# A two-layer mixer in float32: the first layer's second block multiplied plainly, with its y kept on chip

## The chip, the cores and the metric

The kernel runs on one core of one Trainium2 chip. The metric is device time in microseconds (us), lowest is best; the median of three runs of the kernel before is 1554.78 us (1552.35 to 1556.88).

## The reference, cut to what matters

```
for l in range(2):                                  # x: (1, 2048, 1024), float32
    mod = silu(c) @ w_ada[l] + b_ada[l]             # 3 x 1024: shift, scale, gate
    h = rms_norm(x, g_pre[l]) * (1 + scale) + shift
    proj = h @ w_in[l]                              # 1024 x 3072
    u_a, b_a, c_a, gate_a, u_p, gate_p = six slices of proj, 512 wide
    y_a = b_a * conv3(c_a * u_a) * silu(gate_a)     # causal, depthwise
    y_p = pool(u_p, w_pool[l]) * silu(gate_p)       # causal means over 2, 4, 8, 16 tokens, then 128x128 each
    y = concat(y_a, y_p) @ w_out[l]                 # 1024 x 1024
    x = x + gate * rms_norm(y, g_post[l])
```

## The kernel before, in words

Everything is kept transposed: 128 channels on the partitions, tokens along the free axis. The 2048 tokens are two blocks of 1024, so with two layers there are four blocks, (layer, block) = (0,0), (0,1), (1,0), (1,1), done in that order. Each has an **input stage** (h by w_in, with convolution, pooling and gates behind it) and an **output stage** (y by w_out). Float32 operands are split into a high and a low part (float32r), and each product is made of three matmuls: high x high, high x low, low x high (`PASSES`).

- **Plain input stage**, `in_phase`, used for (0,0): 24 column groups of 128, each 8 K-tiles x 3 passes x 2 token halves of 512 = 48 matmuls, 1152 in all. Weights come in halves of four K-tiles; `Weights.load` issues the DMA (SP queue), `high` casts the high part on ACT, `settle` takes the low part on DVE. In turn k = 1 of a half, `settle` does the half that is used two halves later. y stays on chip.
- **Input stage with seven products**, `in_seven`, used for the other three blocks: two column groups, two halves of K and two token halves make a 2 x 2 by 2 x 2 product, done with seven products instead of eight (12 pairs x 7 products x 4 K-tiles x 3 passes = 1008 matmuls). It needs sums of weight quarters (S1 to S4), sums of quarters of h (B, T names), and sums of results on DVE. Its y goes to HBM (`yin`) and is read back. `settle` runs two products ahead.
- **Output stage**, `out_phase`: 384 matmuls; beside them the scaled results go to HBM (`ysp`), and the next block's h operands are prepared (`operands`); the last block has its own, `out_last`. What is left of the output's norm is done by `opening`, at the head of the next input stage: the mean of squares, then `rsqrt_steps` (Ln, Identity and Exp on ACT, three DVE steps of Newton) for each token half.

Beside the matmuls runs a list of background tasks, fed by `Paced`: each turn (8 turns to a column group in `in_phase`, one per product in `in_seven`) gives an equal share of the estimated DVE time of all tasks as credit. At most two tasks are active, and one more task's loads are issued ahead. The tasks are: `sum_task`, which reads the quarters of one weight unit, forms S1 to S4 with their high and low parts and writes them to HBM (`sums`), 24 for each layer; `mix_task`, which multiplies the pooling weights into w_in on PE (8 for each layer); `ada_task` (the conditioning product, on DVE); `x_stat_task` (sum of squares of x for the next block's norm); `finish_tasks` (16 for each block: x plus the normed y, for the block whose output stage has just ended).

Every engine executes its instructions in the order written, so a DVE instruction that waits for a DMA holds all DVE work written behind it. `in_phase` ends with `bg.drain()`: all tasks that are left are emitted before the next stage's first instruction.

```
            tasks += [sum_task(0, n, u, True) for n, u in units]
            tasks += [call_task(lambda: load_wpool(1), 0.1)]
            tasks += [sum_task(1, n, u, True) for n, u in mine("AB")[: 2 * EXTRA[0]]]
            tasks += [mix_task(1, g, n, later) for g in range(NCG) for n in range(2)]
            tasks += [x_stat_task(1, s, k, accs, later) for s in range(NH) for k in range(KT)]
```

These stand behind 6 mixes and 8 ada tasks in (0,0)'s list: 28 sums in all there. (0,1) has 16 finish tasks, 16 ada tasks and 12 sums of layer 1; (1,0) has 8 sums, 16 finish and 8 ada tasks; (1,1) has 16 finish tasks.

Of the kernel before, what the change touches and what calls it, by code (L numbers as in the profile page):

```python
# [10 lines left out]
ALU = mybir.AluOpType  # L11
# [18 lines left out]
EXTRA = (2, 6)  # L30
# [3 lines left out]
def trunk(ctx: ExitStack, tc: tile.TileContext, xt, c, wada, vec, rcp, win, wupt, wpool, wout, out):  # L34
# [305 lines left out]
    def x_stat_task(b, s, k, accs, later):  # L340
# [6 lines left out]
        def steps():  # L347
# [11 lines left out]
            if k == KT - 1:  # L359
                yield from stat_steps(accs.pop(s), (0, b, s), later)  # L360

        return load, steps, E2 * ((k > 0) + (k == KT - 1))
# [39 lines left out]
    def mix_task(l, g, n, later):  # L402
# [7 lines left out]
        def steps():  # L410
# [5 lines left out]
            yield 0.3  # L416
# [5 lines left out]
        return load, steps, 0.3  # L422
# [110 lines left out]
    def in_phase(l, b, hrhs, tasks, later, started, yplaces, wplaces):  # L533
# [70 lines left out]
        order = START_ORDER  # L604
        pss, wss, other_half = started
        first = len(wss)
        work = Work()
        mixes = [mix_task(l, 0, n, later) for n in range(2)]
        for load, _, _ in mixes:
            load()  # L610
        ws = Weights([w_src(l, *order[n], h) for n in range(first, len(order)) for h in range(2)], wplaces)
        uses = [use[order[n][0]](order[n][1], 0, HS, [pss[n]]) for n in range(first)]
        for _ in range(5):
            next(other_half)
        next(uses[0])
        next(uses[1])
        next(uses[2])
        for _ in other_half:
            pass
        for steps in uses:  # L620
            for _ in steps:
                pass
        for part in (range(0, 3), range(3, first)):
# [27 lines left out]
        bg = Paced(tasks, 1, 8 * (len(order) - first) - 6)  # L651
        for n in range(first, len(order)):
# [3 lines left out]
            for k in range(KT):  # L656
# [16 lines left out]
        return lambda k: y[k]  # L673
# [207 lines left out]
    def out_phase(l, b, y, nl, nb, ws, hplaces, lplaces):  # L881
# [61 lines left out]

        def evict(j, ps):
# [21 lines left out]
        ops = [operands(k) for k in range(KH)]  # L966
        ops[0][0]()
        nl_ = 0
        for j in range(KT):
            ps = [bank("ps_out") for _ in range(NH)]  # L970
            for n, k in enumerate(range(KT) if j else OUT_ORDER):
# [8 lines left out]
                if n == 6 and j < KH:  # L980
                    work.q.append(ops[j][1]())
                    if j + 1 < KH:
                        ops[j + 1][0]()
                work.run(free)
# [3 lines left out]
        spare = {}  # L988

        def fill(n, name, k, it=iter(lplaces)):  # L990
# [12 lines left out]
        fills = [fill(n, name, k) for n, name in enumerate(LATE) for k in range(KH)]  # L1003
# [14 lines left out]
        return h, fills, opening  # L1018
# [282 lines left out]

    with working(9, 4, 4, 3, 0):
        with tc.manual_schedule(engines={E.DVE, E.PE, E.Activation}):
            hrhs, started = start(0)
        with tc.manual_schedule():
            later = Later()
            tasks = [mix_task(0, g, n, later) for g in range(1, NCG) for n in range(2)]
# [119 lines left out]
```

## Time and profile before

| what | value |
|---|---|
| median of 3 runs | 1554.78 us |
| the profiled execution | 1560.83 us, span of its instructions 1559.1 us |
| busy, PE / DVE / ACT / POOL | 1403.5 / 1047.8 / 522.1 / 368.3 us |
| mean granted TensorE clock | 0.947 of full speed |
| HBM read / written | 259.09 / 104.33 MB |

The profiled execution lasts 1.7 us longer than its span and stands 6.05 us above the median. PE is TensorE with its matmuls, PEld its weight loads, DVE VectorE, ACT ScalarE, POOL GpSimd, SP the queue that issues most loads. "Busy" is the time in which an engine executes an instruction.

### The profile page before, as it was taken

How to read it: one execution, taken by the hardware profiler on the slowest of the kernel's cores; microseconds unless marked ns; L12 is line 12 of the kernel's file. 1: busy time of each engine (PE TensorE's matmuls, PEld its weight loads, DVE VectorE, ACT ScalarE, POOL GpSimd, SP SyncE). 2: the span in 40 equal slices, each digit the busy share in tenths (PEclk: the TensorE clock that was granted, in tenths of full speed). 3: DMA queues.
4: the chain of work that ended last, by engine and by line, in shares of the span. 5: the costliest groups of instructions: out<-in, count | busy, mean ns of one | idle time of the engine just before them, and what ended most of it. 6: DMA issues, size and time to landing. Idle time of an engine off the chain costs nothing. (4 is left out here: it accounts for less than half of the span.)

```text
span 1559.1 us, 18650 instructions
## 1 busy us (share of the span) xinstructions
PE 1403.5 (90%) x6100; PEld 1139.2 (73%) x6100; DVE 1047.8 (67%) x1763; ACT 522.1 (33%) x928; POOL 368.3 (24%) x535
## 2 busy tenths in 40 slices
PE   8899999945999999768899987999999899999996
PEld 4678888834877777546687776777788688888796
DVE  8954876845757778657675774877775656556555
ACT  4332434334544221222454521222364511112421
POOL 4500344350222221434022333221012122221000
PEclk9999999976999999889999999999999999999998
DMA  7407879786668999688666789878756788687513
GB/s 298 156 21 227 267 268 326 265 299 205 209 218 283 276 313 309 211 280 266 212 223 214 220 282 304 275 256 284 237 198 203 225 236 250 212 251 227 189 63 101
DMA packets 181668, 364.70 MB, mean 234 GB/s; under 512 B 20289, under 2 KB 48961, under 8 KB 181570
## 3 DMA queue, kind: packets, MB, share of 16 engines
q1 hardware_dynamic: 112178, 187.84, 37.0%
q0 software_dynamic: 69392, 175.67, 34.6%
q8 instruction: 48, 0.79, 0.2%
q14 instruction: 50, 0.41, 0.1%
HBM read 259.09 MB, written 104.33 MB: 233 GB/s over the span
## 5 line engine op out<-in xcount | busy, mean ns | idle before, releaser
L792 PE MATMUL ps_in<-h,ws 128*128 128x512 f32 x3024 | 729.2, 403 | 80.9 <-DVE ws L727 73.7
L792 PEld LDWEIGHTS ps_in<-h,ws 128*128 128x128 f32 x3024 | 587.6, 195 | 221.2 <-DVE ws L727 87.4
L388 PE MATMUL ps_out<-y,ws 128*128 128x512 f32 (+1 forms) x1728 | 355.7, 368 | 0.6 <-ACT ws L210 0.6
L388 PEld LDWEIGHTS ps_out<-y,ws 128*128 128x128 f32 x1728 | 300.5, 190 | 55.1 <-ACT ws L210 1.2
L388 PE MATMUL ps_in<-h,ws 128*128 128x512 f32 x816 | 185.9, 389 | 0.0
L388 PEld LDWEIGHTS ps_in<-h,ws 128*128 128x128 f32 x816 | 152.9, 188 | 31.6
L702 POOL DMA_DIRECT2D ws<-sums x144 | 103.7, 730 | 200.4 <-PE ps_in L792 184.7
L210 ACT CAST ws<-raw 128x512 fp32r<-128x512 f32 x98 | 60.1, 623 | 129.4 <-PE ps_out L388 48.6
L388 PE MATMUL ps_in<-h,w 128*128 128x512 f32 x336 | 86.7, 418 | 14.5 <-ACT h L377 8.0
L220 DVE TENSOR_TENSOR ws<-raw,ws 128x512 fp32r<-128x512 f32 x98 | 66.8, 688 | 48.2 <-ACT ws L210 48.1
L727 DVE TENSOR_TENSOR ws<-raw,ws 128x512 fp32r<-128x512 f32 x108 | 74.0, 686 | 29.2 <-ACT ws L717 29.2
L816 ACT COPY v<-ps_in 128x512 f32<-128x512 f32 x36 | 21.2, 590 | 213.1 <-PE ps_in L792 213.1
L388 PEld LDWEIGHTS ps_in<-h,w 128*128 128x128 f32 x336 | 66.8, 202 | 34.3 <-ACT h L377 11.6
L948 POOL DMA_DIRECT2D ysp<-yg x48 | 26.3, 547 | 275.3 <-ACT yg L947 275.3
L717 ACT CAST ws<-raw 128x512 fp32r<-128x512 f32 x108 | 63.1, 620 | 67.2 <-DMA raw<-win 35.0
L837 ACT ACTIVATE second<-second 128x1024 f32<-128x1024 f32 x24 | 25.5, 1062 | 149.5 <-DVE second L831 141.0
L474 POOL DMA_DIRECT2D sums<-raw x96 | 68.2, 773 | 3.9 <-DMA sums<-raw 2.0
L264 DVE SCALAR_TENSOR_TENSOR adaw<-adaw,cb 128x512 f32<-128x512 f32 x64 | 42.7, 688 | 33.6 <-DMA adaw<-wada 31.2
L472 POOL DMA_DIRECT2D sums<-s x48 | 35.4, 738 | 126.3 <-DVE s L467 118.8
L463 ACT CAST s13h<-s 128x512 fp32r<-128x512 f32 x48 | 29.8, 621 | 87.1 <-DVE s L458 41.7
L471 POOL DMA_DIRECT2D sums<-s13h x48 | 39.2, 816 | 72.2 <-ACT s13h L463 49.4
L457 DVE TENSOR_TENSOR s<-raw,raw 128x256 f32<-128x256 f32 x20 | 8.4, 421 | 56.3 <-DMA raw<-win 47.5
(174 smaller groups left out, 1494.9 us busy)
## 6 DMA issues: line engine op xcount, KB each, us to landing
ws<-sums POOLq DMA_DIRECT2D x144, 512.0 KB, 7.6
raw<-win SPq DMA_DIRECT2D x110, 256.0 KB, 5.3
sums<-raw POOLq DMA_DIRECT2D x96, 256.0 KB, 5.0
raw<-win SPq DMA_DIRECT2D x160, 128.0 KB, 4.4
adaw<-wada SPq DMA_DIRECT2D x64, 256.0 KB, 5.0
raw<-wout SPq DMA_DIRECT2D x64, 256.0 KB, 3.9
sums<-s13h POOLq DMA_DIRECT2D x48, 256.0 KB, 5.4
sums<-s POOLq DMA_DIRECT2D x48, 256.0 KB, 4.6
```

The lines of the kernel that those rows point to most:

```text
L210: nc.scalar.copy(self.ws[m][:, 0], self.raws[m].rearrange("p (a b) -> p a b", b=P))
L220: nc.vector.tensor_tensor(t[:, 1], raw, t[:, 0].bitcast(F32), op=ALU.subtract)
L264: nc.vector.scalar_tensor_tensor(w[n], w[n], 1.0, cb[:, n * HS : (n + 1) * HS], op0=ALU.mult, op1=ALU.mult, accum_out=m[:, l, j : j + 1])
L388: nc.tensor.matmul(ps[s], lhsT=ws[k // KH][:, wi, k % KH, :], rhs=rhs(k, ri, s), start=first and (wi, ri) == PASSES[0], stop=last and (wi, ...
L463: nc.scalar.copy(xh, xf)
L471: nc.gpsimd.dma_start(dst[:, 0, 0:4:2, cols].bitcast(F32), xh.bitcast(F32))
L472: nc.gpsimd.dma_start(dst[:, 1, 0:4:2, cols].bitcast(F32), xf)
L474: nc.gpsimd.dma_start(dst[:, :, 1 + 2 * m, cols].bitcast(F32), rs[m].bitcast(F32))
L702: nc.gpsimd.dma_start(ops[m].rearrange("p a b c -> p a (b c)"), sums[l, n][:, :, SUM[a]])
L717: nc.scalar.copy(ops[m][:, 0], raws[m].rearrange("p (a b) -> p a b", b=P))
L727: nc.vector.tensor_tensor(ops[m][:, 1], raw, ops[m][:, 0].bitcast(F32), op=ALU.subtract)
L792: nc.tensor.matmul(ps, lhsT=ops[m][:, wi, k, :], rhs=h[hn][k][:, ri, :], start=p < 4 and k == 0 and (wi, ri) == (0, 0), stop=k == KH - 1 a ...
```

## The change

1. (0,1)'s input stage becomes plain: `in_phase` instead of `in_seven`, so layer 0's 24 weight sums are not made, and y is not sent through HBM. `out_phase` gets a form `plain` in which (0,0)'s output stage prepares the plain h (`plain_operands`), and which fetches the first three weight halves of the input stage to come (`plain.high(3)`, `plain.settle`). `opening` is called in turns 0, 4 and 9 of `in_phase`, and background tasks start after turn 9.
2. Layer 1's sums: 16 (pairs A and B) in (0,0), 8 (pairs P) in (0,1), none in (1,0).
3. Layer 1's 8 mixes move from (0,0) to (0,1). (0,0)'s `x_stat_task`s stand among the sums instead of at the end, and their two means are tasks of their own (`x_stat_end`), with the matmuls five turns later (`later(5, mean)`).
4. In (1,0) the 8 ada tasks are spread between the 16 finish tasks.
5. The buffer pools of (0,0)'s output and (0,1)'s input stage: 8 wide, 6 half, 4 landing, 3 weight buffers; (0,1)'s output stage starts with the pools that `in_seven` uses.

```diff
@@ x_stat_task, stat_steps
-            if k == KT - 1:
-                yield from stat_steps(accs.pop(s), (0, b, s), later)
...
-        yield None
-        yield None
-        xstat[key] = mean_mm((ah, al))
+
+        def mean():
+            xstat[key] = mean_mm((ah, al))
+
+        later(5, mean)
+
+    def x_stat_end(b, s, accs, later):
+        return (lambda: None), (lambda: stat_steps(accs.pop(s), (0, b, s), later)), E2
@@ in_phase
-        bg = Paced(tasks, 1, 8 * (len(order) - first) - 6)
+        bg = Paced(tasks, 1, KT * (len(order) - first) - (10 if started else 20))
...
+                turn = KT * (n - first) + k
+                if opening and turn in (0, 4, 9):
+                    opening((0, 1, 3)[(0, 4, 9).index(turn)])
+                    free = 0
                 free = work.run(free)
-                if free > 0:
-                    bg.run(free + 1)
+                if not opening or turn > 9:
+                    bg.run(free + 1 if free > 0 else 0)
@@ out_phase
+            def steps():
+                t = xs[0]
+                nc.vector.scalar_tensor_tensor(t, t, apre[:, nl, k : k + 1], rn, op0=ALU.mult, op1=ALU.mult)
...
+                    nc.scalar.activation(hp0[s][k][:, 0], u, AF.Identity, bias=mod[:, nl, k : k + 1])
+                yield None
+                for d, u in parts:
+                    prenorm_lo(d[:, 0], d[:, 1], nl, k, u)
+                    yield E2
...
+                if plain and j == KT - 1 and n == 6:
+                    plain.high(3)
+                    plain.settle(2)
@@ the program
             tasks = [mix_task(0, g, n, later) for g in range(1, NCG) for n in range(2)]
-            tasks += [ada_task(0, 2 * KT + k) for k in range(KT)]
-            tasks += [call_task(lambda: ada_fin(0, 2, 0, KT), 0.3)]
-            tasks += [sum_task(0, n, u, True) for n, u in units]
+            rest = [ada_task(0, 2 * KT + k) for k in range(KT)]
+            rest += [call_task(lambda: ada_fin(0, 2, 0, KT), 0.3)]
+            rest += [x_stat_task(1, s, k, accs) for s in range(NH) for k in range(KT)]
+            tasks += between(rest, [sum_task(1, n, u, True) for n, u in mine("AB")])
+            tasks += [x_stat_end(1, s, accs, later) for s in range(NH)]
             tasks += [call_task(lambda: load_wpool(1), 0.1)]
-            tasks += [sum_task(1, n, u, True) for n, u in mine("AB")[: 2 * EXTRA[0]]]
-            tasks += [mix_task(1, g, n, later) for g in range(NCG) for n in range(2)]
-            accs = {}
-            tasks += [x_stat_task(1, s, k, accs, later) for s in range(NH) for k in range(KT)]
...
+    with working(8, 6, 4, 3, 0), tc.manual_schedule():
+        ws = out_weights(0, wplaces)
+        ws.load(3)
+        ws.settle(2)
+        first = in_weights(0, IN_ORDER, 0, wplaces[1:] + wplaces[:1])
+        hrhs, _, opening = out_phase(0, 0, y, 0, 1, ws, hplaces, None, first)
+        later = Later()
+        mixes = [mix_task(1, g, n, later) for g in range(NCG) for n in range(2)]
+        fins = finish_tasks(0, 0, later)
+        adas = [ada_task(1, j) for j in list(range(8, 16)) + list(range(8))]
+        adas += [call_task(lambda: (ada_fin(1, 1, 0, KT), ada_fin(1, 0, 0, KT)), 0.5)]
+        sums_ = [sum_task(1, n, u, True) for n, u in mine("P")]
+        tasks = between(mixes, fins[:4]) + between(between(adas, sums_), fins[4:])
+        y = in_phase(0, 1, hrhs, tasks, later, None, yplaces, first.places, first, opening)
...
-        for n, (l, b) in enumerate(blocks[1:], 1):
+        for n, (l, b) in enumerate(blocks[2:], 2):
...
             if (l, b) == (1, 0):
-                tasks = [sum_task(1, n_, u, False) for n_, u in sorted(rest)[2 * EXTRA[1] :]] + tasks
-                tasks += [ada_task(1, 2 * KT + k) for k in range(KT)]
+                tasks = between(tasks, [ada_task(1, 2 * KT + k) for k in range(KT)])
```

`between(many, few)` spreads the second list evenly through the first. Twenty-four sums are gone from the whole, and 144 matmuls are added.

Where the engines' instructions come to stand is seen in the order in which they are issued. First PE from (0,0)'s last products to (0,1)'s first ones, in the kernel before (ps_wu is a mix, ps_stat a mean, L388 and L792 the plain and the seven-product matmuls):

```order
L388 MATMUL ps_in<-h,ws 128x512 x798
L414 MATMUL ps_wu<-wp,wupt 128x128 x32
L309 MATMUL ps_stat<-ah,ones 128x512
L309 MATMUL ps_stat<-al,ones 128x512
L309 MATMUL ps_stat<-ah,ones 128x512
L309 MATMUL ps_stat<-al,ones 128x512
L388 MATMUL ps_out<-y,ws 128x512 x384
L792 MATMUL ps_in<-h,ws 128x512 x48
```

The same place now (L390 is the plain matmul, L308 the mean):

```order
L390 MATMUL ps_in<-h,ws 128x512 x750
L308 MATMUL ps_stat<-ah,ones 128x512
L308 MATMUL ps_stat<-al,ones 128x512
L390 MATMUL ps_in<-h,ws 128x512 x6
L308 MATMUL ps_stat<-ah,ones 128x512
L308 MATMUL ps_stat<-al,ones 128x512
L390 MATMUL ps_in<-h,ws 128x512 x30
L390 MATMUL ps_out<-y,ws 128x512 x384
L390 MATMUL ps_in<-h,ws 128x512 x60
```

The 32 mix matmuls (eight mixes) and the two means no longer stand between the last product and the output stage; the means stand 36 and 30 matmuls ahead of the end, the mixes among (0,1)'s products.

Second, ACT in `opening` of (1,0), at the head of its input stage (L287, L288 and L289 are Ln, Identity and Exp of one token half; L717 is the cast of a weight quarter, L829 a result). Before:

```order
L184 CAST ah<-acc 128x512 x2
L717 CAST ws<-raw 128x512 x2
L287 ACTIVATE rs_a<-ps_stat,epsc 128x512
L288 ACTIVATE rs_v<-ps_stat,epsc 128x512
L289 ACTIVATE ry<-rs_a 128x512
L287 ACTIVATE rs_a<-ps_stat,epsc 128x512
L288 ACTIVATE rs_v<-ps_stat,epsc 128x512
L289 ACTIVATE ry<-rs_a 128x512
L717 CAST ws<-raw 128x512
L829 COPY u<-ps_in 128x512
L837 ACT_TABLE_LOAD
```

Now (the same operations are L183, L729, L286, L287, L288, L841, L849):

```order
L729 CAST ws<-raw 128x512 x2
L286 ACT_TABLE_LOAD
L286 ACTIVATE rs_a<-ps_stat,epsc 128x512
L287 ACTIVATE rs_v<-ps_stat,epsc 128x512
L288 ACT_TABLE_LOAD
L288 ACTIVATE ry<-rs_a 128x512
L286 ACT_TABLE_LOAD
L286 ACTIVATE rs_a<-ps_stat,epsc 128x512
L287 ACTIVATE rs_v<-ps_stat,epsc 128x512
L288 ACT_TABLE_LOAD
L288 ACTIVATE ry<-rs_a 128x512
L729 CAST ws<-raw 128x512
```

Four loads of an activation table stand among the six activations, ahead of the cast of a weight quarter; before there was none.

Third, ACT where (0,1)'s input stage ends and its output stage begins, now (L599 is the Silu of the last gate, L544 the cast of its y, L209 the cast of an output weight, L875 the table load that `out_phase` asks for):

```order
L209 CAST ws<-raw 128x512 x2
L875 ACT_TABLE_LOAD
L599 ACT_TABLE_LOAD
L599 ACTIVATE sga<-ps_in 128x512 x2
L209 CAST ws<-raw 128x512
L544 CAST y<-cv 128x512 x2
L286 ACT_TABLE_LOAD
L286 ACTIVATE rs_a<-ps_stat,epsc 128x512
L287 ACTIVATE rs_v<-ps_stat,epsc 128x512
L288 ACT_TABLE_LOAD
L288 ACTIVATE rn<-rs_a 128x512
```

The table load of `out_phase` has come ahead of the last Silu, which loads its own table over it; from there on each Ln and each Exp loads a table, up to the place shown second.

## Rows read from the trace of the kernel before

**Rows 1.** The page's first line.

```profile
span 1559.1 us, 18650 instructions
```

**Rows 2.** Stages: start:end, us, busy (x instructions) by engine, granted clock, DMA share, GB/s.

```profile
135.70:317.00 181.30, 181.30 (x804) 150.16 (x804) 143.33 (x300) 66.48 (x142) 66.64 (x95) 1.00 0.85 284
317.00:371.50 54.50, 13.58 (x69) 11.11 (x67) 25.00 (x48) 23.01 (x44) 18.51 (x28) 0.64 0.76 267
371.50:461.90 90.40, 89.69 (x386) 73.71 (x385) 52.40 (x75) 43.18 (x72) 16.85 (x30) 0.97 0.62 210
461.90:764.50 302.60, 253.32 (x1017) 201.52 (x1018) 217.91 (x398) 85.57 (x154) 78.46 (x117) 0.92 0.87 276
...
852.40:1125.00 272.60, 246.08 (x1017) 198.40 (x1018) 198.18 (x344) 80.04 (x142) 66.71 (x101) 0.94 0.85 269
1125.00:1212.90 87.90, 87.19 (x386) 71.91 (x384) 54.97 (x78) 43.77 (x73) 16.91 (x30) 1.00 0.58 192
1212.90:1453.90 241.00, 234.76 (x1012) 191.48 (x1013) 154.86 (x229) 59.87 (x100) 45.24 (x69) 0.99 0.77 234
```

**Rows 3.** PE's timeline: start, length, line, tiles, count, [idle before <- releaser].

```profile
127.66 2.02 PE L414 MATMUL ps_wu<-wp,wupt 128*128 128x128 f32 x16 [1.96 <-DMA wupt<-wupt]
...
135.77 181.16 PE L388 MATMUL ps_in<-h,ws 128*128 128x512 f32 x798
316.76 1.95 PE L414 MATMUL ps_wu<-wp,wupt 128*128 128x128 f32 x16
...
371.47 89.71 PE L388 MATMUL ps_out<-y,ws 128*128 128x512 f32 x384
...
764.48 87.20 PE L388 MATMUL ps_out<-y,ws 128*128 128x512 f32 x384
...
1233.26 208.61 PE L792 MATMUL ps_in<-h,ws 128*128 128x512 f32 x912 [2.94 <-DVE ws L727]
```

**Rows 4.** Groups by line: DVE's work in a sum task.

```profile
L469 DVE TENSOR_TENSOR raw<-raw 128x256 fp32r<-128x256 f32 x96 | 36.2, 420 | 0.0
...
L467 DVE TENSOR_TENSOR s<-s,s13h 128x512 fp32r<-128x512 f32 x48 | 32.9, 685 | 0.0
...
L458 DVE TENSOR_TENSOR s<-raw 128x256 f32<-128x256 f32 x48 | 20.2, 420 | 0.0
```

**Rows 5.** ACT's timeline at the end of (0,0)'s input stage.

```profile
316.74 1.09 ACT L597 ACTIVATE sga<-ps_in 128x512 f32<-128x512 f32 x2 [1.96 <-PE ps_in L388]
```

**Rows 6.** ACT's timeline at the head of (0,0)'s output stage.

```profile
372.08 1.28 ACT L863 ACT_TABLE_LOAD   x1
373.37 0.62 ACT L210 CAST ws<-raw 128x512 fp32r<-128x512 f32 x1
```

**Rows 7.** PE's waits in (0,1): total us, times, longest.

```profile
PE ps_in L792 <- DVE ws L727: 46.1, 15, 7.9
```

**Rows 8.** PE's waits in (1,0).

```profile
PE ps_in L792 <- DVE ws L727: 22.0, 9, 5.2
```

**Rows 9.** PE's waits in (1,1).

```profile
PE ps_in L792 <- DVE ws L727: 5.6, 4, 2.9
```

**Rows 10.** DVE's timeline in (1,0), a finish task.

```profile
974.83 0.69 DVE L1035 TENSOR_TENSOR fin<-fin 128x512 f32<-128x512 f32 x1 [8.05 <-DMA fin<-xt]
```

**Rows 11.** All engines' timeline, `opening` of (1,0).

```profile
864.70 0.69 ACT L287 ACTIVATE rs_a<-ps_stat,epsc 128x512 f32<-128x512 f32 x1
...
870.10 1.28 ACT L837 ACT_TABLE_LOAD   x1
...
871.03 0.69 DVE L281 SCALAR_TENSOR_TENSOR ry<-rs_a,ry 128x512 f32<-128x512 f32 x1
871.63 0.69 DVE L727 TENSOR_TENSOR ws<-raw,ws 128x512 fp32r<-128x512 f32 x1
...
872.37 4.21 PE L792 MATMUL ps_in<-h,ws 128*128 128x512 f32 x9 [3.46 <-DVE ws L727]
```

**Rows 12.** SP's queue behind (0,0)'s last product: x_stat loads.

```profile
344.02 20.45 SPq L345 DMA_DIRECT2D xin<-xt  x16
```

More of the change, by code (lines that the diff above doesn't have):

```diff
@@ L338, in trunk, with x_stat_task @@
     ry = {}
[L340 removed]
+    def x_stat_task(b, s, k, accs):
         t = []
@@ L531, in flush, with in_phase @@
                 self.tick()
-    def in_phase(l, b, hrhs, tasks, later, started, yplaces, wplaces):
+    def in_phase(l, b, hrhs, tasks, later, started, yplaces, wplaces, ws=None, opening=None):
         y = [[None] * NH for _ in range(KT)]
@@ L603, in in_phase @@
         use = {"up": use_up, "gp": use_gp, "ua": use_ua, "ca": use_ca, "ba": use_ba, "ga": use_ga}
-        order = START_ORDER
-        pss, wss, other_half = started
-        first = len(wss)
         work = Work()
[L608 to L621, printed above, removed]
-                pass
-        for part in (range(0, 3), range(3, first)):
+        if started:
+            order = START_ORDER
+            pss, wss, other_half = started
+            first = len(wss)
+            mixes = [mix_task(l, 0, n, later) for n in range(2)]
+            for load, _, _ in mixes:
+                load()
+            ws = in_weights(l, order, first, wplaces)
+            uses = [use[order[n][0]](order[n][1], 0, HS, [pss[n]]) for n in range(first)]
+            for _ in range(5):
+                next(other_half)
+            next(uses[0])
+            next(uses[1])
+            next(uses[2])
+            for _ in other_half:
+                pass
+            for steps in uses:
+                for _ in steps:
+                    pass
+        else:
+            order, first = IN_ORDER, 0
+        for part in (range(0, 3), range(3, first)) if started else ():
             ps1 = {n: bank("ps_in") for n in part} if part[0] == 0 else {}
@@ L672, in in_phase, with in_weights @@
         later.flush()
-        return lambda k: y[k]
+        return y
+    def in_weights(l, order, first, places):
+        return Weights([w_src(l, *order[n], h) for n in range(first, len(order)) for h in range(2)], places)
     PRODUCTS = (
@@ L942, in operands, with plain_operands, load @@
             return load, steps, 0
+        hp0 = [[None] * KT for _ in range(NH)]
+        def plain_operands(k):
+            xs = []
+            def load():
+                xs.append(tmp("xin")[:, :TB])
+                nc.sync.dma_start(xs[0], x_src(nl, k, nb * TB, TB))
+            def steps():
+                t = xs[0]
+                nc.vector.scalar_tensor_tensor(t, t, apre[:, nl, k : k + 1], rn, op0=ALU.mult, op1=ALU.mult)
+                yield E1
+                yield None
+                parts = []
+                for s in range(NH):
+                    hp0[s][k] = slot(next(hp), [P, 2, HS], "h")
+                    u = t[:, s * HS : (s + 1) * HS]
+                    parts.append((hp0[s][k], u))
+                    nc.scalar.activation(hp0[s][k][:, 0], u, AF.Identity, bias=mod[:, nl, k : k + 1])
+                yield None
+                for d, u in parts:
+                    prenorm_lo(d[:, 0], d[:, 1], nl, k, u)
+                    yield E2
+            return load, steps, 0
         def evict(j, ps):
@@ L965, in out_phase @@
         work.q.append(norm())
-        ops = [operands(k) for k in range(KH)]
+        ops = [plain_operands(k) for k in range(KT)] if plain else [operands(k) for k in range(KH)]
         ops[0][0]()
-        nl_ = 0
         for j in range(KT):
@@ L1001, in fill @@
             return load, fin
-        fills = [fill(n, name, k) for n, name in enumerate(LATE) for k in range(KH)]
+        fills = [] if plain else [fill(n, name, k) for n, name in enumerate(LATE) for k in range(KH)]
         st = {}
@@ L1300, in out_weights, with between @@
         return Weights([wout[l, j][:, n * KH : (n + 1) * KH] for j in range(KT) for n in range(2)], places, raw)
+    def between(many, few):
+        r, n = [], len(few)
+        for i, t in enumerate(many):
+            r.append(t)
+            r += few[i * n // len(many) : (i + 1) * n // len(many)]
+        return r
     with working(9, 4, 4, 3, 0):
```

30 lines of the change are left out of this document (13 added, 17 removed).

## The prediction, as it was recorded before the result

> **What bounds the kernel now.** I read the span, then the table of stages, then PE's timeline where stages meet, then the waits inside the stages, and last ACT and DVE at the two places where the order of instructions changes. The sum is made against the profiled execution: 1559.1 us of span and 1.7 us around it, 1560.8 us [rows 1].
>
> The table of stages [rows 2] shows PE as the bound, but not everywhere to the same degree. (0,0)'s products run without a gap: 181.3 us busy of 181.3, granted clock 1.00. Then come 54.5 us in which PE is busy for 13.6 us and DVE for 25.0, at a clock of 0.64, between the levels of 1.2 and 2.4 GHz: background tasks left over, which `bg.drain()` puts ahead of the next stage. (0,1) takes 302.6 us for the same 1008 matmuls for which (1,1) takes 241.0; (1,0) lies between with 272.6. The timeline gives the price of a matmul without waits [rows 3]: 181.16/798 = 0.227 us plain, 87.20/384 = 0.227 us in an output stage, 208.61/912 = 0.229 us with seven products. So 1008 cost 230.5 us, and (0,1) loses 72 us, (1,0) 42, (1,1) 10.5. The waits say where: PE waits for DVE's low part of a weight for 46.1 us in (0,1), 22.0 in (1,0), 5.6 in (1,1) [rows 7, 8, 9]. The rest is the slower clock after each gap: 0.92, 0.94, 0.99 [rows 2]. DVE isn't full there (218 of 303 us). It is held by loads: a finish task waits 8.05 us for its x [rows 10], and the weight's low part stands behind it. The three blocks differ in their tasks: 12 sums, 16 finish and 16 ada tasks; 8, 16 and 8; 16 finish tasks.
>
> **Part by part.**
>
> *The tail of (0,0).* Twelve of 28 sums go, eight mixes move away, and the means stand among the last products. A sum costs DVE four operations of 0.42 us, one of 0.685 and two of 0.377 (36.2/96), 3.1 us [rows 4]. DVE was busy for 143.3 + 25.0 = 168.3 us in the products and the tail; without twelve sums 131 of 181 us, so the tasks fit. What is left behind the last product (316.9) is the last gate: two Silus of 1.09 us together [rows 5], then the cast of the first output weight, 0.62 us by [rows 6]. With a few tenths for semaphores, and 1 us for the two means that now lie in PE's stream, the output stage begins at about 319.8 instead of 371.5: **-51.7 us**. Its y comes two DVE and ACT steps later, but is multiplied last. Bounds: 318 (the gate covered as well) and 337. The upper one keeps 54.5 - 12 x 3.1 = 17 us of tail, if the tail only shrinks by the DVE time of the sums.
>
> *(0,0)'s output stage* took 90.4 us at clock 0.97, the others 87.9 at 1.00 [rows 2]. After a 2 us gap I take 88.5: **-1.9**. The plain operands cost DVE less than those that they replace, and hide as they did.
>
> *(0,1) plain.* 1152 matmuls at 0.227 are 261.6 us; eight mixes, two of which take 1.95 us with overlap and 1.7 from start to start [rows 3], add 7.0; eight mean matmuls 2; the gap at the start 0.7, as at the seven-product stages. The stalls of `in_seven` I take as gone: the plain stage needs a low part seven turns of 1.36 us after its turn, 9.5 us, where `in_seven` leaves two products of 2.75. The longest of DVE's waits on a finish task is 8 us [rows 10], and (0,0), with a heavier list, ran 798 matmuls without a gap. Where PE itself waits is a mix whose load is late: 1.96 us once for six mixes [rows 3]; the eight stand apart, so I take 2.4 in all, with bounds of 0 and 8 x 1.96 = 16. Together 273.7 instead of 302.6: **-28.9**, bounds 268 and 290.
>
> *(0,1)'s output stage.* Its weights' first casts and two table loads stand ahead of the last Silu, in time in which ACT waits for PE, so they hide. Four more loads then delay the norm by about 2 us against before; the output weights have two halves of 5.4 us in hand: **+0.5**, bounds 0 and 3.
>
> *(1,0).* Without 8 sums and with the ada tasks spread, the list asks 45 us of DVE's credit over 69 turns, where it was 70, and 22 in (1,1). I start from (1,1), 241.0; add 1 us for the two means of x, 4 us for some waits on finish loads that remain (a tenth of its 42 us of loss), and the new table loads. In `opening` the low part of a weight stands on DVE behind the second Newton chain, which stands behind the second Exp on ACT: 864.70 the first Ln, 871.03 the last Newton step, 871.63 the low part, 872.37 PE after 3.46 us of waiting [rows 11]. Nothing is slack on that chain, so four loads of 1.28 us ahead of the second Exp lengthen the wait by 5.1, to 8.6. Against (1,1), whose wait there is 2.94 [rows 3], that is +5.7. Sum 251.7: **-20.9**, bounds 243 (loads and remaining waits hidden) and 263 (three tenths of the old loss kept).
>
> The row on table loads decides their price: the load at 372.08 lasts 1.28 us and the next cast starts at 373.37, at its end [rows 6]. The Trainium skill, ScalarE: Activation LUTs, section What ACT_TABLE_LOAD costs, says that a switch costs 1283 ns of load and some 1380 ns of drain; the rows agree with the first figure and show no time for the second here. By it the wait would grow by 10.6 us instead of 5.1. The same page, section Table sets: the hidden batching unit, says that Ln and then Exp need one load, since one set has both. By it the term would be 1.3 us; but the order shows four loads written out, so this kernel switches sets.
>
> (1,1) and the last output stage keep their work: 0. Sum: -51.7 - 1.9 - 28.9 + 0.5 - 20.9 = **-102.9 us**. 1560.8 - 102.9 = 1457.9 for a profiled execution. The one of before stood 6.05 us over the median 1554.8; taken off, **1452 us**.
>
> **The rivals.**
>
> *The list doesn't clear in time (0.15).* 17 us of tail stay in (0,0), and each mix waits for its load in (0,1), 13 us more than I took. For: one task is loaded ahead, and fewer landing buffers stand in (0,1). Against: DVE has 50 us free in (0,0). 1452 + 17 + 13 = 1482.
>
> *All covered (0.12).* The table loads and the remaining waits of (1,0) hide, and no mix waits: 1452 - 5.1 - 4 - 2.4 = 1440. For: (1,1) shows 912 matmuls in a row with the same finish tasks. Against: the chain of [rows 11] has no slack.
>
> *A table load holds ACT twice as long as its row (0.05).* Then `opening` waits 5.1 us more, and (0,1)'s output stage, whose norm is delayed by another 5 us, waits some 2: 1459. For it speaks no row; [rows 6] is against it. This is the drain of the page above.
>
> *Slower than before (0.04).* Loads set the pace of the tasks, with one task ahead. (0,0) has 50 tasks in the 193 us between 124 and 317, (0,1) 49 in 260: 4.6 us each. If each took over 453/99 + 103/99 = 5.6 us on average, the tails would give back all of the gain: at 5.7, 1452 + 99 x 5.7 - 453 = 1563. For: the wait of 8.05 us [rows 10]. Against: sixteen x_stat loads are issued in 20.45 us [rows 12], 1.3 us each, and finish tasks in (1,1) keep their pace without holding PE.
>
> That the change doesn't do what it says is excluded: the order shows the mixes and means moved.
>
> **How the numbers follow.** The forecast has 0.64, the rivals 0.15, 0.12, 0.05 and 0.04. The predicted time is the forecast's 1452. The range goes from 1433, where (0,1) and (1,0) stand at their lower bounds (-5.7, -8.7) and the gate is covered (-2) with 2 us for the spread of the runs, to 1487, the first rival with the spread of a measurement on top; it leaves out the slower case and combinations of upper bounds. Faster by more than 0.3%, about what a measurement of this kernel can tell from no change, is every case but the slower one, 0.95; within 0.3% 0.01; slower 0.04.
>
> **What would show it.** Right: no more than 3 us of idle PE between (0,0)'s last product and the output stage; (0,1)'s input stage at 270 to 280 us, clock 1.00, without waits for DVE's low parts; in `opening` of (1,0) four table loads and a wait of PE of 8 to 9 us; (1,0) near 252. Wrong: ten or more us of DVE work behind (0,0)'s last product; waits of PE for DVE in the plain stage, or for mixes at each of eight places; (1,0) still above 263, which would mean that finish tasks alone hold DVE.

## The result and the profile after

The changed kernel took 1445.2 us, median of 4 runs (1441.8 to 1447.0), beside 1555.8 us for the kernel before (1552.4 to 1557.5) on the same chip: a ratio of 0.929 (95% interval 0.927 to 0.931), 110.7 us less. The prediction was 1452, between 1433 and 1487. The profiled execution took 1441.8 us, 119.0 less than the profiled one of before, where the sum said 102.9. The profiled execution of before stands 5.0 us above the median of its kernel here and this one 3.4 below, so 8.4 of the 119.0 us are the choice of executions.

From the head of the page of the changed kernel: span, and what the DMA engines moved.

```profile
span 1440.0 us, 17843 instructions
...
DMA packets 143116, 291.23 MB, mean 202 GB/s; under 512 B 15921, under 2 KB 32305, under 8 KB 143026
```

The kernel before moved 364.70 MB. The page shows 20% fewer bytes for 144 more matmuls; the experiments come back to the stores among them.

The table of stages of the changed kernel: start:end, us, then busy time (and instructions) of PE, PE's weight loads, DVE, ACT and POOL, then granted clock, DMA share, GB/s.

```profile
137.50:316.90 179.40, 179.40 (x793) 148.25 (x791) 129.11 (x257) 66.92 (x135) 46.52 (x66) 1.00 0.69 236
316.90:318.40 1.50, 0.05 (x2) 0.02 (x1) 0.54 (x1) 1.50 (x4) 0.00 (x0) 1.00 0.00 0
318.40:406.05 87.65, 87.49 (x385) 72.12 (x385) 46.63 (x63) 41.40 (x70) 7.58 (x14) 1.00 0.43 144
406.05:676.40 270.35, 270.35 (x1225) 224.97 (x1224) 169.94 (x310) 86.21 (x157) 36.93 (x58) 1.00 0.59 193
...
764.30:1008.25 243.95, 234.14 (x1017) 191.48 (x1017) 175.28 (x288) 75.78 (x122) 45.18 (x69) 0.99 0.80 248
...
1096.20:1335.00 238.80, 233.08 (x1013) 190.74 (x1014) 154.81 (x229) 59.64 (x100) 45.12 (x69) 0.99 0.76 235
```

Against [rows 2]: the 54.5 us behind (0,0)'s products are 1.5 us. (0,1)'s input stage, now plain, has PE busy for all of its 270.35 us at clock 1.00, where it took 302.6 at 0.92. (1,0) takes 243.95 instead of 272.6, and (1,1) 238.8 instead of 241.0. The DMA rate fell in the three stages that make fewer sums: 284 to 236 GB/s in (0,0), 276 to 193 in (0,1), 269 to 248 in (1,0).

PE's timeline where the stages meet: start, length, line, tiles, count, [idle before <- releaser].

```profile
318.38 1.20 PE L390 MATMUL ps_out<-y,ws 128*128 128x512 f32 x4 [1.45 <-ACT ws L209]
319.74 86.47 PE L390 MATMUL ps_out<-y,ws 128*128 128x512 f32 x380 [0.16 <-DVE ws L219]
...
788.80 110.20 PE L804 MATMUL ps_in<-h,ws 128*128 128x512 f32 x478 [7.81 <-DVE ws L739]
899.30 92.82 PE L804 MATMUL ps_in<-h,ws 128*128 128x512 f32 x408
...
1115.37 208.65 PE L804 MATMUL ps_in<-h,ws 128*128 128x512 f32 x912 [2.46 <-DVE ws L739]
```

The output stage of (0,0) starts 1.45 us behind the last product; the forecast left about 2. In (1,0) only the opening has a long wait. PE's waits in (1,0) after the change (total us, times, longest), which answer to [rows 8]:

```profile
PE ps_in L804 <- DVE ws L739: 9.7, 4, 7.8
PE ps_in L804 <- ACT ws L729: 0.7, 1, 0.7
```

22.0 us of waiting for DVE became 9.7, and 7.8 of that is the opening. For (0,1) the same view lists no wait of PE at all, where [rows 7] had 46.1 us. The chain of the opening stands in ACT's timeline:

```profile
776.87 1.28 ACT L286 ACT_TABLE_LOAD   x1
778.17 0.69 ACT L286 ACTIVATE rs_a<-ps_stat,epsc 128x512 f32<-128x512 f32 x1
...
779.45 1.28 ACT L288 ACT_TABLE_LOAD   x1
780.75 0.63 ACT L288 ACTIVATE ry<-rs_a 128x512 f32<-128x512 f32 x1
781.39 1.28 ACT L286 ACT_TABLE_LOAD   x1
...
785.27 0.63 ACT L288 ACTIVATE ry<-rs_a 128x512 f32<-128x512 f32 x1
```

and in DVE's:

```profile
787.45 0.69 DVE L280 SCALAR_TENSOR_TENSOR ry<-rs_a,ry 128x512 f32<-128x512 f32 x1
788.06 0.69 DVE L739 TENSOR_TENSOR ws<-raw,ws 128x512 fp32r<-128x512 f32 x1
```

From the first Ln to the low part is 788.06 - 778.17 = 9.89 us, where it was 871.63 - 864.70 = 6.93 [rows 11]; with the first load ahead of it 11.2. PE starts 0.74 us after the low part begins, as before.

### The profile page after: what moved, and what is told of

It reads as the page before. It is cut to its first block, busy times and chain, and to the rows that moved or that the text cites. A ratio compares the mean times of both kernels' runs of the same rounds, so it can differ in the third digit from the quotient of the medians.

```text
span 1440.0 us, 17843 instructions
## 1 busy us (share of the span) xinstructions
PE 1391.7 (97%) x6244; PEld 1142.8 (79%) x6244; DVE 932.5 (65%) x1519; ACT 500.9 (35%) x869; POOL 256.9 (18%) x372
## 2 busy tenths in 40 slices
DMA packets 143116, 291.23 MB, mean 202 GB/s; under 512 B 15921, under 2 KB 32305, under 8 KB 143026
## 5 line engine op out<-in xcount | busy, mean ns | idle before, releaser
L804 PEld LDWEIGHTS ps_in<-h,ws 128*128 128x128 f32 x2016 | 379.9, 189 | 100.5 <-DVE ws L739 19.7
L390 PE MATMUL ps_in<-h,ws 128*128 128x512 f32 x1968 | 450.6, 390 | 0.0
L390 PEld LDWEIGHTS ps_in<-h,ws 128*128 128x128 f32 x1968 | 368.7, 188 | 76.0
L390 PE MATMUL ps_out<-y,ws 128*128 128x512 f32 (+1 forms) x1728 | 353.7, 367 | 2.2 <-ACT ws L209 2.0
L390 PEld LDWEIGHTS ps_out<-y,ws 128*128 128x128 f32 x1728 | 298.7, 189 | 56.6 <-ACT ws L209 2.9
L209 ACT CAST ws<-raw 128x512 fp32r<-128x512 f32 x146 | 89.6, 622 | 300.5 <-PE ps_in L390 144.9
L219 DVE TENSOR_TENSOR ws<-raw,ws 128x512 fp32r<-128x512 f32 x146 | 99.6, 688 | 115.8 <-ACT ws L209 112.8
L390 PE MATMUL ps_in<-h,w 128*128 128x512 f32 x336 | 86.8, 418 | 14.3 <-ACT h L379 7.2
L714 POOL DMA_DIRECT2D ws<-sums x96 | 67.5, 704 | 185.4 <-PE ps_in L804 171.8
L390 PEld LDWEIGHTS ps_in<-h,w 128*128 128x128 f32 x336 | 66.8, 201 | 33.6 <-ACT h L379 9.6
L739 DVE TENSOR_TENSOR ws<-raw,ws 128x512 fp32r<-128x512 f32 x72 | 49.3, 685 | 17.6 <-ACT ws L729 17.6
L729 ACT CAST ws<-raw 128x512 fp32r<-128x512 f32 x72 | 41.5, 620 | 24.0 <-PE ps_out L390 17.7
L263 DVE SCALAR_TENSOR_TENSOR adaw<-adaw,cb 128x512 f32<-128x512 f32 x64 | 42.8, 685 | 10.7 <-DMA adaw<-wada 9.0
L849 ACT ACTIVATE second<-second 128x1024 f32<-128x1024 f32 x16 | 17.0, 1062 | 93.1 <-DVE second L843 90.2
L995 DVE TENSOR_TENSOR acc<-acc,sq 128x512 f32<-128x512 f32 x42 | 28.9, 692 | 24.9 <-ACT sq L992 24.9
L473 POOL DMA_DIRECT2D sums<-s13h x24 | 18.0, 748 | 147.3 <-ACT s13h L465 123.1
L843 DVE TENSOR_TENSOR second<-ps_in,v 128x512 f32<-128x512 f32 x16 | 11.1, 692 | 44.4 <-PE ps_in L804 44.4
L1083 POOL DMA_DIRECT2D x<-fin x32 | 18.8, 586 | 116.6 <-DVE fin L1078 113.8
L1076 DVE TENSOR_TENSOR fin<-fin,ry 128x512 f32<-128x512 f32 x48 | 32.8, 684 | 6.0 <-DMA fin<-ysp 6.0
```

The lines of the kernel that those rows point to most:

```text
L209: nc.scalar.copy(self.ws[m][:, 0], self.raws[m].rearrange("p (a b) -> p a b", b=P))
L219: nc.vector.tensor_tensor(t[:, 1], raw, t[:, 0].bitcast(F32), op=ALU.subtract)
L263: nc.vector.scalar_tensor_tensor(w[n], w[n], 1.0, cb[:, n * HS : (n + 1) * HS], op0=ALU.mult, op1=ALU.mult, accum_out=m[:, l, j : j + 1])
L390: nc.tensor.matmul(ps[s], lhsT=ws[k // KH][:, wi, k % KH, :], rhs=rhs(k, ri, s), start=first and (wi, ri) == PASSES[0], stop=last and (wi, ...
L714: nc.gpsimd.dma_start(ops[m].rearrange("p a b c -> p a (b c)"), sums[l, n][:, :, SUM[a]])
L729: nc.scalar.copy(ops[m][:, 0], raws[m].rearrange("p (a b) -> p a b", b=P))
```

## The experiments

The theory at first was that of the prediction: time goes where DVE's work and the low parts of weights behind it are late, and the sums cost what they hold DVE, with little lead in a seven-product stage. The rivals were the order of the tasks, the table loads as the only late thing, and later the transfers themselves. Each kernel from experiment 4 on ran once, so these are read by their stages, not by their totals. "Dummy" sums below are `sum_task`s of layer 0, as the kernel before made them, put back into the changed kernel: they write sums that nothing reads.

**1. The changed kernel again**, with no edit, as the base of experiments 2 and 3.

> The changed kernel again, on the same chip as the two kernels that come next, for a comparison within one per cent. Both theories: about 1445 us, ratio to before 0.929; in the profile, PE waits 7.8 us in the opening of (1,0).

Median 1446.9 us (1444.1 to 1448.5), ratio 0.930 (0.927 to 0.932). (1,0) took 245.1 us, its opening waited 7.8 again. Between kernels whose instructions are the same up to there, the start of (0,0)'s output stage moves from 318.4 to 322.6 us, and the difference lies before the stretch of 750 matmuls that begins at 137.5 to 141.7; so a difference of 4 us or less between two single executions says nothing.

**2. The nine extra table loads taken away.** `log_exp()`, which preloads the table with Ln and Exp, moves from the head of `out_phase`, where a Silu still follows, to the norm.

```diff
@@ out_phase
-        log_exp()
...
         def norm():
+            log_exp()
             for s in range(NH):
```

> The table load that the output stage asks for is issued as the first step of its norm, so it can't come ahead of the last Silu; the nine extra table loads go. Theory (the four loads in the opening of (1,0) lie on the path): that wait of PE falls from 7.8 to about 2.7 us, and the time by 5 us against the changed kernel, about 1440. Rival (the loads lie beside other work, and the wait has another cause): the wait stays at 6 us or more and the time within 1.5 us.

Median 1439.8 us (1437.0 to 1441.7), 7.1 below experiment 1, by intervals that just touch (ratios 0.923 to 0.927 and 0.927 to 0.932). PE's waits in (1,0):

```profile
PE ps_in L804 <- DVE ws L739: 5.0, 4, 3.0
```

The opening waits 3.0 us instead of 7.8, and (1,0) takes 240.3 instead of 245.1: 4.8 us for the four loads in front of the second Exp. So they set that wait, as predicted.

**3. More lead for the low parts**, on top of experiment 2.

```diff
-    LOAD, HIGH, SETTLE = 6, 3, 2
+    LOAD, HIGH, SETTLE = 6, 4, 3
```

The cast and the low part of a weight are made three products ahead of their use instead of two.

> As the kernel with the table load in the norm, and in the seven-product stages the cast and the low part of a weight are done one product earlier (HIGH 4, SETTLE 3). Theory (PE waits in the openings and closings of (1,0) and (1,1) because low parts come at most two products ahead): the waits of 2.5 and some of 1.4 us in these two stages shrink, another 5 us less, about 1435. Rival (the low parts then only queue elsewhere on DVE): no change against the kernel with the table load alone, within 1.5 us.

Median 1429.9 us (1428.6 to 1431.9), ratio 0.919 (0.917 to 0.921): 17.0 us below experiment 1, and faster than both kernels by intervals that don't meet. (1,0) is 233.3 us, (1,1) 234.0. PE's only waits for DVE that the seven-product matmuls have left in the whole kernel, and the window of (1,0) (columns as in the table of stages):

```profile
PE ps_in L804 <- DVE second L838: 2.9, 3, 1.2
```

```profile
767.75:1001.00 233.25, 231.57 (x1016) 190.50 (x1017) 173.85 (x288) 69.86 (x117) 45.30 (x69) 1.00 0.83 258
```

No PE wait for a low part is left. So the lead does matter, by some 5 to 7 us for a seven-product stage that has few tasks.

**4. The same lead in the kernel before.** This asks whether lead alone would have saved what (0,1) lost there.

```diff
@@ the kernel before
-    LOAD, HIGH, SETTLE = 6, 3, 2
+    LOAD, HIGH, SETTLE = 6, 4, 3
```

> The kernel before, with the cast and the low part of a weight one product earlier in the seven-product stages (HIGH 4, SETTLE 3), nothing else. Theory (these stages lose their time because the low part has only two products, 5.5 us, in hand when DVE is held by a load, where the plain stage has 9.5): 15 waits of 3 us in (0,1) and 9 of 2.4 in (1,0) each lose up to 2.75 us; (0,1) falls from 302.6 to about 275, (1,0) from 272.6 to about 255, the whole to 1505 to 1525. Rival (DVE's or the loads' throughput is the bound there, not the lead): both stages within 5 us of before.

1520.5 us. The windows of (0,1) and (1,0):

```profile
458.70:750.80 292.10, 250.16 (x1017) 197.78 (x1018) 217.39 (x398) 85.30 (x154) 78.02 (x117) 0.93 0.89 287
...
838.70:1091.50 252.80, 239.60 (x1016) 194.61 (x1017) 194.84 (x342) 79.03 (x141) 66.64 (x101) 0.97 0.89 287
```

PE's longest waits in (0,1):

```profile
PE ps_in L792 <- DVE second L826: 13.2, 3, 8.1
PE ps_in L792 <- ACT s13h L463: 9.8, 1, 9.8
PE ps_in L792 <- DVE second L822: 5.4, 4, 4.4
PE ps_in L792 <- DVE ws L727: 4.8, 5, 1.5
```

The theory, which had forecast some 275 us for (0,1) and 255 for (1,0), holds in half. The waits for low parts fell from 46.1 us [rows 7] to 4.8, and (1,0) came down by 19.8. But (0,1) lost only 10.5 of its 72 us, because PE now waits for other things, a sum's ACT step for 9.8 us among them. Both stages, 292 and 253 us long and with different tasks, run at the same 287 GB/s with a DMA share of 0.89. From here on the transfers were a rival: a stage with many sums may last as long as its bytes take to move.

**5. Twelve dummy sums in (0,0)**, as many as the change takes out.

```diff
-            tasks += between(rest, [sum_task(1, n, u, True) for n, u in mine("AB")])
+            tasks += between(rest, [sum_task(1, n, u, True) for n, u in mine("AB")] + [sum_task(0, n, u, True) for n, u in units[:12]])
```

> The changed kernel with 12 sums of layer 0 made again in (0,0) (written to HBM, read by nobody), so that (0,0) makes 28 as before. Theory (the tail of before was DVE time: too many sums for the stage): a tail between the last product and the output stage comes back, 5 to 17 us. Rival (the tail came from the order, with mixes and sums of squares standing last): no tail, the output stage starts within 2 us of the changed kernel's 318.4.

1469.6 us. The window from the last mix to the last product, and PE's waits in it:

```profile
137.50:338.90 201.40, 186.24 (x797) 149.15 (x795) 163.68 (x342) 79.82 (x170) 80.71 (x114) 0.99 0.89 307
```

```profile
PE ps_in L390 <- DVE ws L219: 8.9, 7, 1.8
PE ps_in L390 <- ACT ws L209: 5.1, 4, 2.9
```

The output stage starts at 340.5 instead of 318.4, 22.1 us later, and not because of a tail: the products themselves wait, 14 us in all by these two rows. DVE is busy for 164 of 201 us. The transfers run at 307 GB/s with a share of 0.89, against 236 and 0.69 without the sums. Both forecasts missed, that of a tail of 5 to 17 us and that of no cost.

**6. The x_stat tasks behind the sums again**, where the kernel before had them.

```diff
-            rest += [x_stat_task(1, s, k, accs) for s in range(NH) for k in range(KT)]
             tasks += between(rest, [sum_task(1, n, u, True) for n, u in mine("AB")])
+            tasks += [x_stat_task(1, s, k, accs) for s in range(NH) for k in range(KT)]
```

> The changed kernel with the 16 sums of squares of (0,0) behind the weight sums again, as before, and no more sums than the changed kernel has. Theory (DVE time): the output stage starts within 3 us of 318.4. Rival (order): some 20 us of tail, as long as these tasks took in the tail of before.

1449.5 us; the output stage starts 1.46 us behind the last product, as in the changed kernel. With the short list, the place of these 16 tasks costs nothing. With 28 sums it was not tried, so the rival that it was the order falls only for these tasks and this list.

**7. Eight dummy sums in (0,1)**, the plain stage.

```diff
+        sums_ += [sum_task(0, n, u, True) for n, u in units[16:24]]
```

> The changed kernel with 8 sums of layer 0 added to the tasks of (0,1), 16 sums there (written, read by nobody). Theory (the plain stage has 9.5 us in hand for a low part and hides such tasks): (0,1) stays at 270.4 us within 2, and PE doesn't wait for DVE. Rival (what (0,1) gained is that it has fewer tasks): 15 us or more are added.

1452.9 us. The window of (0,1)'s input stage:

```profile
410.40:682.60 272.20, 270.88 (x1225) 224.91 (x1224) 191.82 (x366) 95.49 (x181) 59.69 (x90) 1.00 0.71 238
```

It takes 272.2 us instead of 270.35. In the plain stage, whose transfers had room, eight sums cost 1.9 us together, and PE never waits for DVE.

**8. Eight dummy sums in (1,0)**, the seven-product stage, where the kernel before had eight.

```diff
+                tasks = [sum_task(0, n_, u, False) for n_, u in units[16:]] + tasks
```

> The changed kernel with 8 sums of layer 0 put at the head of the tasks of (1,0), where 8 sums stood before (written, read by nobody). Theory (in a seven-product stage a sum that waits for its load holds the low parts, and PE): (1,0) goes from 243.9 to 265 to 272 us. Rival (8 sums are 25 us of DVE time in a stage where DVE has 70 us free, and cost nothing; the gain of (1,0) came from the spread ada tasks): under 250.

1473.4 us. The window of (1,0)'s input stage, then DVE's longest waits for loads in it:

```profile
768.10:1037.60 269.50, 243.24 (x1016) 195.91 (x1017) 197.69 (x344) 85.22 (x146) 66.69 (x101) 0.95 0.85 272
```

```profile
DVE s L459 <- DMA raw<-win: 20.4, 3, 10.3
DVE fin L1076 <- DMA fin<-ysp: 11.6, 6, 4.6
```

Sums of the same eight weight units that cost 1.9 us in (0,1) cost 25.6 here, which is about all that (1,0) had lost before. They aren't quite the same tasks: here they stand at the head of the list and each lands in two of the six landing buffers, which the finish and ada tasks use too; in (0,1) they are spread through the list and land in one wide buffer (the last argument of `sum_task`). DVE waits for the loads of sums and of finish tasks; in the changed kernel the four longest waits of DVE in this stage, 20.8 to 7.3 us in total, are all for PE or ACT. The loads themselves are issued late. SP issues them in its order, and these are its waits at the load of a sum (L451) for the store of an earlier sum (`sums<-raw`), which holds the buffer; in (1,0) here, then in (0,1) of experiment 7:

```profile
SPq L451 <- DMA sums<-raw: 48.8, 6, 15.7
```

```profile
SPq L451 <- DMA sums<-raw: 0.3, 1, 0.3
```

**9. All 24 dummy sums**: twelve in (0,0), four in (0,1), eight in (1,0), by the edits of experiments 5, 7 (`units[12:16]`) and 8 together.

> The changed kernel with all 24 sums of layer 0 made again, shared out as before: 28 sums in (0,0), 12 in (0,1), 8 in (1,0) (those of layer 0 are read by nobody). Theory (the parts add: 22 us in (0,0), about 1 in (0,1), 26 in (1,0)): 49 us over the changed kernel, about 1492 to 1497; so of the change's 110 us some 60 come from multiplying (0,1) plainly and from the new order of (0,0)'s tasks, and some 50 from sums that aren't made. Rival (the sums disturb one another's loads across stages): over 60 us more, above 1505.

1494.7 us. The windows of (0,0), from the last mix to the output stage, and of (1,0):

```profile
140.40:343.40 203.00, 186.49 (x799) 149.14 (x797) 164.80 (x343) 81.34 (x174) 80.66 (x114) 0.99 0.88 305
...
789.40:1059.70 270.30, 241.58 (x1016) 194.26 (x1017) 197.37 (x344) 84.71 (x146) 66.48 (x101) 0.96 0.84 271
```

The parts add up: 203.0 - (179.4 + 1.5) = 22.1 us in (0,0), 26.4 in (1,0), and nothing in (0,1) (270.4 us). So some 49 of the 110.7 us (49.5 by this one run's total, 48.5 by its stages) are sums that are no longer made; the other 61 or so are (0,1) plain and what else changed for (0,0)'s tasks: the mixes moved away, the x_stat tasks stand among the sums, and the pacing. Of that last, no run was made.

**10. The ada tasks of (1,0) behind the finish tasks again.**

```diff
-                tasks = between(tasks, [ada_task(1, 2 * KT + k) for k in range(KT)])
+                tasks += [ada_task(1, 2 * KT + k) for k in range(KT)]
```

> The changed kernel with the 8 ada tasks of (1,0) behind the 16 finish tasks, as before, instead of between them. Theory (without the sums the credit per turn is low enough for finish tasks either way, so what the sums cost is all of the gain of (1,0)): (1,0) within 3 us of 243.9 to 246.3. Rival (finish tasks back to back hold DVE on their loads, and the spread removed that): 250 us or more.

1449.5 us, with 246.1 us in (1,0). Five executions in which (1,0) is as the change made it took 243.9 to 246.3 us there (the changed kernel and experiments 1, 5, 6 and 7), so no effect of spreading the tasks is shown; (1,0)'s gain is the sums.

**11. Eight dummy sums in (1,0) with the longer lead**: experiment 3 and experiment 8 together.

> The kernel with the table load in the norm and low parts one product earlier (233.3 us in (1,0)), with 8 sums of layer 0 at the head of the tasks of (1,0), as in the run that put them into the changed kernel and cost 25.6 us there. Theory (what a sum costs there is the part of DVE's wait on its load that exceeds the lead of the low parts): with 2.75 us more lead the same 8 sums cost 10 to 18 us, (1,0) 243 to 251. Rival (they cost DVE or DMA throughput): 23 us or more again.

1455.0 us. The window of (1,0):

```profile
766.50:1025.60 259.10, 241.02 (x1017) 193.85 (x1017) 195.83 (x343) 78.93 (x141) 66.90 (x101) 0.97 0.87 281
```

259.1 instead of 233.3: 25.8 us, the same price as with the short lead. Here the theory of lead falls: what a sum costs in this stage doesn't come from low parts that stand too close to their use.

**12. All 24 dummy sums, their four stores left out.** DVE's and ACT's work and the loads of a sum stay; the sum isn't written.

```diff
-    def sum_task(l, n, u, wide):
+    def sum_task(l, n, u, wide, store=True):
...
-            nc.gpsimd.dma_start(dst[:, 0, 0:4:2, cols].bitcast(F32), xh.bitcast(F32))
-            nc.gpsimd.dma_start(dst[:, 1, 0:4:2, cols].bitcast(F32), xf)
-            for m in range(2):
-                nc.gpsimd.dma_start(dst[:, :, 1 + 2 * m, cols].bitcast(F32), rs[m].bitcast(F32))
+            if store:
+                nc.gpsimd.dma_start(dst[:, 0, 0:4:2, cols].bitcast(F32), xh.bitcast(F32))
+                nc.gpsimd.dma_start(dst[:, 1, 0:4:2, cols].bitcast(F32), xf)
+                for m in range(2):
+                    nc.gpsimd.dma_start(dst[:, :, 1 + 2 * m, cols].bitcast(F32), rs[m].bitcast(F32))
```

> The run with all 24 sums of layer 0 back (203 us from the last mix to the output stage in (0,0), 270.4 us in (0,1), 270.3 in (1,0)), but those 24 sums, which nobody reads, are not stored: all their work on DVE and ACT and their loads stay, two thirds of their bytes go (1 of 1.5 MB each). Theory DVE (the predicted one: sums cost DVE time and hold low parts behind their loads): (0,0) still at 198 us or more, (1,0) at 262 or more, the whole within 12 us of 1495. Theory DMA (a stage with sums carries 271 to 307 GB/s and is bound by the bytes; behind full queues every load comes late): (0,0) back to 181 to 186, (1,0) to 244 to 252, the whole at 1445 to 1460.

1458.1 us, 36.6 below experiment 9. The same two windows:

```profile
138.00:330.30 192.30, 184.73 (x798) 149.70 (x796) 163.71 (x343) 81.24 (x173) 46.51 (x66) 0.99 0.76 256
...
777.90:1024.80 246.90, 235.66 (x1017) 191.71 (x1018) 197.78 (x344) 84.95 (x146) 45.13 (x69) 0.98 0.83 263
```

DVE is as busy as with the stores (163.7 and 197.8 us against 164.8 and 197.4). In (1,0) the stage takes 246.9 us, 1 to 3 us more than without any dummy sum (243.9 to 246.3): there DVE's work and the loads of the sums are nearly free, and the stores carry the price. In (0,0) the stage is between the forecasts of the two theories (181 to 186, and 198 or more): the stores carry 10.7 of the 22.1 us, and the rest belongs to the loads, DVE or ACT, and no run divides it further.

## Why the prediction was right, and what in it was not

**(0,0)'s tail, -51.7.** The output stage starts at 318.4, after 371.5: -53.1 us. The gap of 1.45 us is the Silus and the first weight's cast, as the forecast had it; the rival with 17 us of tail is refuted. Most of the tail before was PE waiting for the mixes and the means that stood in it behind the last sums (317.0 to 371.5 us):

```profile
PE ps_wu L414 <- ACT wk L419: 20.6, 3, 17.5
PE ps_stat L309 <- ACT ah L366: 20.4, 2, 12.9
```

Both have moved, and with 28 sums again no tail returns (experiment 5). So the sums are 22.1 of the 53.1 us, and the other 31 go with the moved mixes, the x_stat tasks and the pacing together. The pacing is a part of the change that the prediction doesn't weigh: (0,0)'s list is spread over four turns fewer, and a turn without room now adds to the credit, where it was passed over before. No run takes these three apart. The size came out right, in part by luck: the reasoning that DVE has time for its tasks (131 of 181 us) isn't what decides. By the same arithmetic twelve more sums would have fitted as well (129.1 + 12 x 3.1 = 166 of 181 us), and experiment 5 shows that they cost 22 us, inside the products and without a tail. The 3.1 us of DVE time that the upper bound charged for a sum is not the price of one.

**(0,0)'s output stage, -1.9.** -2.7 us, at clock 1.00.

**(0,1) plain, -28.9.** -32.2 us: 270.4 us against 273.7. No mix waited for its load, for which the sum had 2.4; that is most of the difference. Experiment 4 corrects the reason, though. The prediction said that the stalls go because the plain stage keeps a low part 9.5 us ahead of its use where `in_seven` keeps 5.5. A lead of three products in the kernel before gave (0,1) only 10.5 us, so lead alone is not it, and that the size came out is in part luck. The stage also moves fewer bytes now, 270.35 x 193 = 52.2 MB instead of 302.6 x 276 = 83.5. Experiment 7 gives it part of them back (238 GB/s), and it hardly slows. How a seven-product (0,1) without sums would do was not tried, so what the stalls of (0,1) came from stays open between lead, sums and bytes.

**(0,1)'s output stage, +0.5.** 0: 87.9 us before and after. The two table loads ahead of the last Silu stand in time in which ACT waits for PE, as the timeline of ACT shows:

```profile
671.35 1.28 ACT L875 ACT_TABLE_LOAD   x1
672.63 1.28 ACT L599 ACT_TABLE_LOAD   x1
...
676.41 1.09 ACT L599 ACTIVATE sga<-ps_in 128x512 f32<-128x512 f32 x2 [2.49 <-PE ps_in L390]
```

**(1,0), -20.9, the term that was mis-sized most.** It measured -28.7, 243.9 us against 251.7. The opening came as worked out: 7.81 us of waiting, 8.6 predicted, with the four loads written out, and experiment 2 gives 4.8 us back for removing them. Of each load the rows show 1.28 us and the next instruction 0.02 us later. The Trainium skill, ScalarE: Activation LUTs, section What ACT_TABLE_LOAD costs, names some 1380 ns of drain beside the load; by an estimate from it the wait would have grown by 10.6 us. It grew by 4.35, and no row here shows such time. What failed is "4 us for some waits on finish loads that remain (a tenth of its 42 us of loss)". Hardly any remained: beside the opening's 7.8 us PE waits 9.7 + 0.7 - 7.8 = 2.6 us in the whole stage, and the 886 matmuls behind the opening took (110.20 + 92.82)/886 = 0.229 us each, as in (1,1). Another 2.2 us are its base, (1,1), which took 238.8 us instead of 241.0. The prediction took the loss of 42 us as one of finish tasks that hold DVE, and thought it would shrink with DVE's credit. Experiments 8, 11 and 12 show that the sums carry it, and of the sums the stores, while DVE's work counts for 1 to 3 us. With the sums gone the waits for finish loads went too.

**(1,1), 0.** -2.2 us. But the changed kernel and experiments 1, 5, 6 and 7, whose edits leave this stage alone, took 238.8 to 241.9 us for it, so no gain is shown.

So the sum of -102.9 was short by 16 us between the profiled executions, by some 8 between the medians; the 16 are: 7.8 of it in (1,0), 3.3 in (0,1), 2.2 in (1,1), 1.4 in the tail, 0.8 and 0.5 in the output stages. The rival that goes to the other side, loads that set the pace of the tasks, did not come: both lists cleared without a tail.

**What stays open.** The stores of a sum take three things: bytes (a dummy sum without them moves 0.53 MB, from (303.84 - 291.23)/24, and with them 1.57, from (329.03 - 291.23)/24), issues on POOL, and the landing buffers that stay held until a store is done. Experiment 12 removes all three at once. What the loads of weights took from issue to landing in the windows above (count, KB each, median us) tells the two stages apart. In (0,0): the changed kernel, experiment 5, experiment 12.

```profile
raw<-win SPq DMA_DIRECT2D x22, 256.0 KB, 3.2
raw<-win SPq DMA_DIRECT2D x22, 256.0 KB, 4.9
raw<-win SPq DMA_DIRECT2D x22, 256.0 KB, 3.5
```

In (1,0): the changed kernel, experiment 8.

```profile
raw<-win SPq DMA_DIRECT2D x27, 256.0 KB, 6.1
raw<-win SPq DMA_DIRECT2D x27, 256.0 KB, 5.5
```

In (0,0) the loads of weights land later with the stores, which speaks for the bytes. In (1,0) these loads land no later with the dummy sums than without; what is late is their issue, for SP's queue stands 48.8 us at buffers that stores still hold, with the loads of weights behind it. That speaks for the buffers and the order of the queue, although the y halves of the finish tasks (`fin<-ysp`) did land later, 6.9 us instead of 5.4, and although in experiment 12 SP stands 36.7 us at the same place, for DVE, and the stage hardly slows. No run kept the bytes and freed the buffers, and that the rates of 269 to 307 GB/s are a ceiling was not shown.

## What to carry to other kernels

A scheme that saves matmuls by sums made beforehand pays for their loads, their stores and the buffers that these hold. So before blaming the engine that PE waits for, read how long loads take to land and what the queue that issues them waits for: here late loads appeared as waits for DVE or ACT, and a longer lead bought nothing of a sum's price (25.8 us against 25.6). The DMA share alone doesn't tell: at 0.85, (0,0) of the kernel before ran its products without a gap [rows 2], and (1,0) of experiment 8 stalled. A background task of one kind cost 0.2 us in one stage and 3.2 in another (1.9/8 and 25.6/8), so try it elsewhere, and in other buffers, before making it shorter. Near a border between stages, read the table loads in ACT's emitted order: of nine extra ones the four at the place where the chain had no slack cost 4.8 us here, and others stood in time that was free anyway.

## What the runs showed of the hardware that was not expected

After the same gap of about 1.5 us the first ten microseconds of (0,0)'s output stage had the granted clock at 1.00 in some executions and at 0.83, between the levels of 1.2 and 2.4 GHz, in others. The windows of experiment 7:

```profile
321.20:331.20 10.00, 9.84 (x35) 7.67 (x36) 7.86 (x12) 6.76 (x11) 0.00 (x0) 0.83 0.43 133
```

and of experiment 8, whose instructions up to there are the same:

```profile
322.20:332.20 10.00, 9.84 (x42) 7.83 (x43) 7.82 (x12) 6.74 (x11) 0.00 (x0) 1.00 0.43 139
```

The output stage takes 89.2 us in the one case and 87.65 in the other; of the eleven experiments with the changed order five had the slower one. That is 1.6 us for a gap whose length didn't differ, so a term such as the prediction's 88.5 for this stage can't be set closer than that.
